# The matmuls of the convolution's LayerNorm sums, two steps further down in TensorE's queue

## The chip, the cores and the metric

The kernel runs on one core of a Trainium2 chip. The metric is the device time of one execution in microseconds (us), lower is better. TensorE (PE in the profile) does the matmuls, VectorE (DVE), ScalarE (ACT) and GpSimd (POOL) the elementwise work, and SyncE (SP) issues the weight loads. Each engine takes its own instructions in the order in which the program wrote them.

## The reference, cut to what matters

Two layers over 256 tokens of width 2048. Layer 0 mixes retention heads and latent attention heads. Layer 1, where the change lies, is a convolution module:

```python
def layer_conformer_conv(x, norm_g, w_in, conv_w, conv_b, ln_g, ln_b, w_out):
    h = rms_norm(x, norm_g)
    a, b, gate = jnp.split(h @ w_in, 3, axis=-1)
    u = a * jax.nn.sigmoid(b)
    u = causal_depthwise_conv_31(u, conv_w) + conv_b      # 31 taps per channel
    u = jax.nn.silu(layer_norm(u, ln_g, ln_b))            # mean and variance over 2048 channels
    return x + (u * jax.nn.silu(gate)) @ w_out
```

The LayerNorm needs, for each token, the sum and the sum of squares over all 2048 channels of the convolution's output. Only then can the first column of the last product, `@ w_out`, be worked out.

## The kernel before, in words

Everything is held with channels on the partitions and tokens along the free dimension: 16 blocks of 128 channels by 256 tokens. Each float32 product is done as three matmuls on rounded parts (`mm3`, L190 to L195): high weight by high activation, high weight by low activation, low weight by high activation. So every weight block has to be split on the chip: ScalarE writes the rounded part `whi` (`hi_to`, L161), and VectorE or GpSimd writes the remainder `wlo` (`lo_to`, L171). The buffers are rings: 3 of `raw` (the loaded weights), 5 of `whi`, 4 of `wlo`.

**Steps.** The weights come in halves of a 1 MB unit. `Stream.half` (L180) is called ahead of each half. It writes the instructions for the remainder `wlo` three halves ahead and for `whi` four halves ahead, then sets the kernel's own clock to the next whole number and lets due work run (`tick`, L108). In the middle of a half a second tick advances it by another half (`tick(True)`), and due work can come there too. One half feeds 24 matmuls of 128x128 by 128x256. In this text one half is called a step. A wlo buffer three steps ahead reuses the one that the step before the present one has read, so its VectorE instruction can start only when TensorE has finished that step.

**Delayed work.** `later(n, fn)` (L102) puts a function down for n steps after now. Each `tick` runs what has come due, ordered by due time and then by the order of putting down, and so writes its instructions into the engines' queues at that place. The order of the queues on TensorE, ScalarE and VectorE is thus written by hand, by such lags.

**The stretch around the change.** While TensorE works out the 16 pairs of `a` and `b` columns and then the 8 pairs of gate columns (`pair`, L352, four steps each, loop at L1096), VectorE runs the convolution's 31 taps per block (L91) as a background, a few at each tick (`pace`, L919). When the last block is done, `centre_add` (L950) adds it to the running sums, writes the result to `sums` (in tile `e`), and puts down `norm_conv` for `LN_LAG` steps later (L958).

`norm_conv` (L984) has two matmuls by a matrix of ones, L986 and L987, that add the 128 partitions up. They are float32, recorded as two passes each. Behind them come the mean, the variance and the reciprocal root on VectorE and ScalarE (from L989 on, `rs_chain`, with a table load at L994). Then 8 pairs of blocks j = 0 to 7 go through five stages each, half a step apart, and pair j starts 2j steps after `norm_conv`:

```python
def za(j): ...  # DVE: subtract the mean, multiply by the root (two instructions)
def zs(j): ...  # ACT: silu with gain and bias (L1008, two instructions)
def zb(j): ...  # DVE: multiply by the gate
def zr(j): ...  # ACT: rounded part zh (L1017)
def zc(j): ...  # DVE: remainder zl
for j in range(8):
    later(2 * j, lambda j=j: z_run(j, 0))
```

After the last pair of gate columns the output projection begins. Its first part is a group of 16 steps with 8 column blocks held at once (`kgroup` on `u_co1`, L1129): step k multiplies by block k of z, so it needs pair j = k//2. The first block's matmuls are lines L345 and L348, the others L193 to L195 into `aux`. `z_need` (L1044) would write missing stages at once; it writes none here if the lags have already brought them. The second part (`u_co2`, pairs again) has 8 x 4 steps of matmuls over all 16 blocks, with the adds and stores at the end.

The steps are numbered from the start of that group: step 0 is its first, steps -4 to -1 are the last gate pair (pair 7), -8 to -5 the pair before it (pair 6). In the kernel before, the sums are written at the tick that opens step -7, and `norm_conv` comes due 2.5 steps later, in the middle of step -5, with 12 + 4 x 24 = 108 matmuls between it and step 0. At the end of a pair, `norm_cols` (L1066) multiplies its result by the RMS factor on VectorE, and the gate's silu on ScalarE follows one step later. A gate that comes due after the sums are written and before `norm_conv` is held until `norm_conv` runs (L1105), so that the ScalarE tables aren't changed in between.

Of the kernel before, what the change touches and what calls it, by code (L numbers as in the profile page):

```python
# [27 lines left out]
TAP_US = 0.396  # L28
TICK_US = 2.88
X1_US = 5.0  # L30
LN_LAG = 2.5
WARM = 9
ENG = {mybir.EngineType.PE, mybir.EngineType.Activation, mybir.EngineType.DVE}
MAGIC = 12582912.0
# [14 lines left out]
def body(ctx, tc, a):  # L49
# [52 lines left out]
    def later(n, fn):  # L102
        due.append((clock[0] + n, len(due), fn))
# [846 lines left out]
    def centre_add(c, m):  # L950
# [4 lines left out]
        if c == 15:  # L955
            lnexp()
            held.append([])
            later(LN_LAG, norm_conv)  # L958

# [267 lines left out]
```

## Time and profile before

| what | value |
|---|---|
| time, median of 3 runs | 840.26 us (838.32 to 843.09) |
| the profiled execution's own time | 839.34 us |
| its span, first to last instruction | 837.6 us |
| granted TensorE clock, mean | 0.995 |
| TensorE's longest wait | 4.3 us, at L986 |

The span and all rows of the trace belong to the one profiled execution. Outside its span lie 839.34 - 837.6 = 1.74 us. The timeline lists instructions by start, length, engine and line; several of a kind in a row are merged with a count, and an idle time ahead of an instruction stands in brackets with what ended it.

### The profile page before, as it was taken

What the parts mean: (1) busy time and instruction counts of PE and PEld (TensorE: products, weight loads), DVE (VectorE), ACT (ScalarE), POOL (GpSimd) and SP (SyncE); (2) the same over time, 40 slices, a digit from 0 to 9 for tenths busy, and PEclk for the clock granted to TensorE, in tenths of its full rate; (3) what the DMA queues carried; (4) which work ended last, traced back from release to release, by engine and by line L of the source; (5) the groups of instructions that cost most, each with busy time, mean ns of one, the idle gap of its engine ahead of it and who ended that gap; (6) DMA issues with size and microseconds to landing.
All of it is one profiled execution on the core that took longest, in us unless ns stands there. A gap on an engine that the chain in (4) does not pass through costs nothing.

```text
span 837.6 us, 16060 instructions
## 1 busy us (share of the span) xinstructions
PE 826.2 (99%) x6592; PEld 814.5 (97%) x6592; DVE 632.5 (76%) x1151; ACT 422.0 (50%) x593; POOL 207.5 (25%) x115
## 2 busy tenths in 40 slices
PE   9999999999999999999999999999999999799998
PEld 8999999999999999999999999999999999799998
DVE  5887565798587755765666399999999999898542
ACT  6766444556455554754545544434444543576330
POOL 0000000000000000000001888885988884000000
PEclk9999999999999999999999999999999999899999
DMA  8965554434545344655444555553555555355650
GB/s 263 350 242 177 185 187 166 151 133 174 197 138 187 133 147 137 218 200 203 171 168 164 201 193 168 195 189 114 201 202 200 177 178 178 125 182 195 228 176 26
DMA packets 24122, 151.16 MB, mean 180 GB/s; under 512 B 2801, under 2 KB 3953, under 8 KB 6897
## 3 DMA queue, kind: packets, MB, share of 16 engines
q1 hardware_dynamic: 23616, 148.03, 51.1%
q0 software_dynamic: 288, 2.10, 0.7%
q8 instruction: 51, 0.84, 0.4%
q14 instruction: 23, 0.18, 0.1%
q10 hardware_dynamic: 144, 0.03, 0.0%
HBM read 148.04 MB, written 2.10 MB: 179 GB/s over the span
## 4 chain that ended last, share of the span: by engine, by line
PE 76%; DVE 20%; issue 1%; ACT 1%; DMA 1%; POOL 1%; SPq 0%; DVEq 0%; POOLq 0%; ACTq 0%
PE mm L195 22%; PE mm L193 22%; PE mm L194 22%; DVE aux L91 13%; DVE mm L88 2%; DVE s L88 2%; PE aux L195 2%; PE aux L194 2%; PE aux L193 2%; DVE wlo L88 1%; DVE t L88 1%; DMA raw<-in_w_first 1%; POOL wlo L88 1%; ACT whi L167 0%; PE aux L641 0%
## 5 line engine op out<-in xcount | busy, mean ns | idle before, releaser
L193 PE MATMUL mm<-s,whi 128*128 128x256 f32 x1788 | 511.0, 286 | 0.5 <-ACT whi L167 0.5
L195 PE MATMUL mm<-s,wlo 128*128 128x256 f32 x1788 | 507.2, 284 | 1.8 <-POOL wlo L88 1.0
L194 PE MATMUL mm<-s,whi 128*128 128x256 f32 x1788 | 506.6, 283 | 0.0
L167 ACT ACTIVATE whi<-raw 128x1024 fp32r<-128x1024 f32 (+2 forms) x278 | 283.2, 1034 | 200.7 <-PE mm L194 121.1
L195 PEld LDWEIGHTS mm<-s,wlo 128*128 128x128 f32 x1788 | 343.7, 192 | 2.9 <-DVE wlo L88 1.6
L193 PEld LDWEIGHTS mm<-s,whi 128*128 128x128 f32 x1788 | 343.8, 192 | 1.5 <-ACT whi L167 0.7
L194 PEld LDWEIGHTS mm<-s,whi 128*128 128x128 f32 x1788 | 343.9, 192 | 0.8
L88 DVE TENSOR_TENSOR wlo<-raw,whi 128x1024 fp32r<-128x1024 f32 (+2 forms) x194 | 229.4, 1193 | 87.3 <-PE mm L195 52.3
L88 POOL TENSOR_TENSOR wlo<-raw,whi 128x1024 fp32r<-128x1024 f32 x84 | 201.9, 2415 | 44.5 <-ACT whi L167 21.9
L91 DVE SCALAR_TENSOR_TENSOR aux<-s,cb,aux 128x256 f32<-128x256 f32 x478 | 198.6, 481 | 11.7 <-ACT aux L872 9.0
L691 POOL MEMSET s<- 64x256 f32 x8 | 2.9, 361 | 232.6 <-PE mm L195 162.7
L193 PE MATMUL mm<-whi,s 128*128 128x272 f32 (+1 forms) x184 | 59.3, 322 | 0.0
L194 PE MATMUL mm<-wlo,s 128*128 128x272 f32 (+1 forms) x184 | 58.9, 320 | 0.0
L195 PE MATMUL mm<-whi,s 128*128 128x272 f32 (+1 forms) x184 | 58.8, 319 | 0.0
L195 PEld LDWEIGHTS mm<-whi,s 128*128 128x128 f32 x184 | 34.6, 188 | 2.3
L193 PEld LDWEIGHTS mm<-whi,s 128*128 128x128 f32 x184 | 34.7, 189 | 1.8
L194 PEld LDWEIGHTS mm<-wlo,s 128*128 128x128 f32 x184 | 34.6, 188 | 1.8
L193 PE MATMUL aux<-s,whi 128*128 128x256 f32 x120 | 34.0, 283 | 0.0
L194 PE MATMUL aux<-s,whi 128*128 128x256 f32 x120 | 34.0, 283 | 0.0
L195 PE MATMUL aux<-s,wlo 128*128 128x256 f32 x120 | 34.0, 283 | 0.0
L1076 ACT ACTIVATE t<-mm 128x256 f32<-128x256 f32 x16 | 6.1, 384 | 54.9 <-DVE mm L88 54.9
L855 POOL MEMSET s<- 128x30 f32 x16 | 1.1, 121 | 119.4 <-PE mm L195 103.6
(186 smaller groups left out, 574.8 us busy)
## 6 DMA issues: line engine op xcount, KB each, us to landing
raw<-in_c_in SPq DMA_DIRECT2D x48, 1024.0 KB, 4.9
raw<-in_w_in SPq DMA_DIRECT2D x36, 1024.0 KB, 4.9
raw<-in_w_out SPq DMA_DIRECT2D x16, 1024.0 KB, 4.9
raw<-in_c_out SPq DMA_DIRECT2D x16, 1024.0 KB, 4.8
raw<-in_w_rv SPq DMA_DIRECT2D x8, 1088.0 KB, 5.0
raw<-in_w_kvb SPq DMA_DIRECT2D x4, 1024.0 KB, 4.9
raw<-in_w_first SPq DMA_DIRECT2D x7, 512.0 KB, 5.5
raw<-in_w_qb SPq DMA_DIRECT2D x3, 1024.0 KB, 4.9
```

Source lines behind the costliest of these rows:

```text
L88: (eng or V).tensor_tensor(out=out, in0=in0, in1=in1, op=op)
L91: V.scalar_tensor_tensor(out=out, in0=in0, scalar=s, in1=in1, op0=op0, op1=op1)
L167: act(hi[:, :], self.raw[u][:, h * n:(h + 1) * n], AF.Copy)
L193: mm(ps, lh, rh, start=start, stop=False, skip_group_check=True)
L194: mm(ps, lh, rl, start=False, stop=False, skip_group_check=True)
L195: mm(ps, ll, rh, start=False, stop=stop, skip_group_check=True)
L691: G.memset(krz(i)[64 * b:64 * b + 64, :], 0.0)
L855: G.memset(upad(c, 0, TAPS - 1), 0.0)
L1076: act(sg[0][:, 0:T], ps[:, T:512], AF.Sigmoid)
```

## The change

One constant, the lag between the writing of the sums and `norm_conv`, goes from 2.5 to 4.5 steps:

```diff
 TAP_US = 0.396
 TICK_US = 2.88
 X1_US = 5.0
-LN_LAG = 2.5
+LN_LAG = 4.5
 WARM = 9
```

`norm_conv` now comes due in the middle of step -3 in place of the middle of step -5. With it move all that it writes or puts down: the two sum matmuls, the chain behind them on VectorE and ScalarE, and all five stages of the 8 pairs. What is put down elsewhere keeps its place: the taps, the sums, `norm_cols`, the splitting of the weights. The gate of pair 6 comes due in the middle of step -4, which is now ahead of `norm_conv`, so it is held and written right behind the chain.

## The prediction

> **What bounds the kernel now.** The first view is the page's head with the busy times.
>
> ```profile
> span 837.6 us, 16060 instructions
> PE 826.2 (99%) x6592; PEld 814.5 (97%) x6592; DVE 632.5 (76%) x1151; ACT 422.0 (50%) x593; POOL 207.5 (25%) x115
> ```
>
> TensorE sets the time: 11.4 us of 837.6 are left uncovered. So only what makes TensorE wait or run slowly counts. The second view is TensorE's waits from 690 us on, and the third the windows around the one wait that it lists (columns: stretch, length, busy time and count of PE, PEld, DVE, ACT, POOL, then granted clock, DMA share, GB/s).
>
> ```profile
> PE aux L986 <- DVE e L88: 4.3, 1, 4.3
> 720.60:725.10 4.50, 0.25 (x3) 0.04 (x2) 3.92 (x9) 0.86 (x3) 0.00 (x0) 0.84 0.49 206
> 725.10:731.00 5.90, 5.90 (x25) 5.54 (x26) 4.21 (x7) 3.94 (x5) 0.00 (x0) 0.54 0.51 178
> ```
>
> TensorE stands 4.3 us at the sum matmuls, until VectorE has written the sums. The wait has a second price: the mean clock of 0.84 over the wait means that it went to one half for (1 - 0.84) / 0.5 x 4.5 = 1.4 us of it, so it fell at 723.7, 2.8 us after the last matmul. In the next window 0.54 means half speed for (1 - 0.54) / 0.5 x 5.9 = 5.4 us after the restart. The fourth view is TensorE's timeline.
>
> ```profile
> 720.44 0.28 PE L194 MATMUL mm<-s,whi 128*128 128x256 f32 x1
> 720.56 0.28 PE L195 MATMUL mm<-s,wlo 128*128 128x256 f32 x1
> 725.09 1.22 PE L986 MATMUL aux<-e,ones 128*128 128x256 f32 x2 [4.25 <-DVE e L88]
> ...
> 726.60 0.78 PE L193 MATMUL mm<-s,whi 128*128 128x256 f32 x1
> ...
> 729.95 0.41 PE L195 MATMUL mm<-s,wlo 128*128 128x256 f32 x1
> 730.16 0.41 PE L193 MATMUL mm<-s,whi 128*128 128x256 f32 x1
> ...
> 741.47 2.08 PE L345 MATMUL aux<-s,whi 128*128 128x256 f32 x16
> ```
>
> Starts are 0.12 us apart at full clock and 0.21 at half; a step of 24 is 24 x 0.12 = 2.88 us. Step 0, the first that needs z, starts at 741.47. The fifth view is VectorE's timeline from the last taps to the first z.
>
> ```profile
> 720.71 1.22 DVE L88 TENSOR_TENSOR wlo<-raw,whi 128x1024 fp32r<-128x1024 f32 x1
> ...
> 725.06 0.42 DVE L88 TENSOR_TENSOR e<-mm,t 128x256 f32<-128x256 f32 x1
> 725.40 1.22 DVE L88 TENSOR_TENSOR wlo<-raw,whi 128x1024 fp32r<-128x1024 f32 x1
> 727.43 1.22 DVE L88 TENSOR_TENSOR wlo<-raw,whi 128x1024 fp32r<-128x1024 f32 x1 [0.81 <-ACT whi L167]
> 728.57 0.41 DVE L989 TENSOR_SCALAR t<-aux 128x256 f32<-128x256 f32 x1
> ...
> 732.42 0.68 DVE L88 TENSOR_TENSOR s<-s,t 128x512 f32<-128x512 f32 x1
> 733.14 0.69 DVE L88 TENSOR_TENSOR s<-s,e 128x512 f32<-128x512 f32 x1
> 733.75 0.69 DVE L88 TENSOR_TENSOR mm<-mm,R 128x512 f32<-128x512 f32 x1
> 734.35 1.21 DVE L88 TENSOR_TENSOR wlo<-raw,whi 128x1024 fp32r<-128x1024 f32 x1
> 735.48 0.68 DVE L88 TENSOR_TENSOR s<-s,s 128x512 f32<-128x512 f32 x1
> 736.08 1.22 DVE L88 TENSOR_TENSOR wlo<-raw,whi 128x1024 fp32r<-128x1024 f32 x1
> 737.22 0.68 DVE L88 TENSOR_TENSOR s<-s,t 128x512 f32<-128x512 f32 x1
> 737.93 0.69 DVE L88 TENSOR_TENSOR s<-s,e 128x512 f32<-128x512 f32 x1
> 738.55 0.68 DVE L88 TENSOR_TENSOR s<-s,s 128x512 fp32r<-128x512 f32 x1
> ```
>
> The reader sees a VectorE that is hardly idle: between these rows it stood for 0.81 us, and otherwise ran one instruction after the other or the chain behind L989. By the order in which the program writes them, the remainders at 720.71, 725.40, 727.43, 734.35 and 736.08 are those for steps -4, -3, -2, -1 and 0. The sums end at 725.06 + 0.42 = 725.48. The last row is zc of pair 0: z for step 0 is there at 738.55 + 0.68 = 739.23, and TensorE comes for it at 741.47, only 2.2 us later. So TensorE's wait in front of L986 hides a second lateness of VectorE, and that is what the change lays open.
>
> **The change, part by part.** TensorE first. Its stall at 720.7 goes: the 12 matmuls left in step -5 run from 720.68, step -4 from 722.12 to 725.00 (its remainder is there at 720.71 + 1.22 = 721.93). Step -3 starts at 725.00, but its third matmul, at 725.24, needs the remainder that ends at 725.40 + 1.22 = 726.62. A new wait of 1.4 us, then, shorter than the 2.8 us after which the clock fell above, so I take no clock loss for it. Ten more matmuls bring TensorE to the sum matmuls at 727.9; the sums have been there since 725.48. These took 726.60 - 725.09 = 1.5 us at half clock; at full clock I take half of it, 0.75. Then 60 matmuls are left to step 0, 60 x 0.12 = 7.2 us. TensorE arrives at step 0 at 727.9 + 0.75 + 7.2 = 735.8, or 736.6 if the sums still take 1.5. That is 5.6 us earlier than 741.47, which is the gross gain: the 4.3 us of waiting, and 2.7 us of half clock, less the 1.4 us.
>
> Now VectorE, with the new order in its queue. Nothing is different up to 727.43. Behind that remainder came the chain; now there stand ahead of it three instructions that came later before: the `norm_cols` of pair 6 (734.35 - 733.75 = 0.60), the remainder of step -1 (735.48 - 734.35 = 1.13) and that of step 0 (737.22 - 736.08 = 1.14). Their inputs are ready: step -5 ends at 722.1, and ScalarE has room for the rounded parts, as its timeline shows.
>
> ```profile
> 726.34 2.00 ACT L167 ACTIVATE whi<-raw 128x1024 fp32r<-128x1024 f32 x2
> ...
> 732.44 1.06 ACT L167 ACTIVATE whi<-raw 128x1024 fp32r<-128x1024 f32 x1
> 733.87 1.09 ACT L1008 ACTIVATE s<-s,cb 128x256 f32<-128x256 f32 x2 [0.36 <-DVE s L88]
> 734.87 0.57 ACT L1102 ACTIVATE s<-mm 128x512 f32<-128x512 f32 x1
> ```
>
> Two rounded parts end at 728.3, two more at 1.0 each at 730.4, and the loads for them were made before. So L989 starts at 728.57 + 0.60 + 1.13 + 1.14 = 731.4, where it was at 728.57. The chain up to za takes 732.42 - 728.57 = 3.85: za at 735.3. za takes 733.75 - 732.42 = 1.33: 736.6. The remainder of step 1 follows, 1.13: 737.8. zs on ScalarE needs za (ready at 736.7) and stands behind the chain's table load (the rounded part behind it started at 732.44 before, so the load ends 2.87 us later than that, at 735.3), the held gate (0.57) and a rounded part (1.06): it starts at 736.9 and ends at 738.0. zb 0.60: 738.6. The remainder of step 2, 1.13: 739.7. za of pair 1, 738.55 - 737.22 = 1.33: 741.1. zc of pair 0, 0.68: 741.75. So z for step 0 comes at 741.75, 2.5 us later than before, because two more remainders (steps 1 and 2) stand in front of it. TensorE, there at 735.8, waits until 741.75, with one matmul (the one that needs only zh) let through a little sooner. Against 741.47 + 0.12, where the second matmul of step 0 ran before, that is **+0.15 us**: the whole gross gain is gone at step 0.
>
> The new wait is 5.9 us, longer than the 4.25 us one. The clock fell 2.8 us into that one, so here too; and I take the same 5.4 us of half speed after the restart, as this is the only such restart in the trace. Step 0 then costs 24 x (0.21 - 0.12) = **+2.2 us**. The bounds: nothing if the clock holds, and 2.2 for a longer half speed as well, since what of it falls into step 1 is hidden by the next part.
>
> A second new cost is in steps 1 to 12. Pair j's zc is now written in the middle of step 2j - 1 and needed at step 2j; before there were two and a half steps between. On VectorE there stand ahead of it the remainder for three steps on, which cannot start before TensorE has finished step 2j - 2, and za of the next pair. The trace of before shows just that sequence, at the beginning of its step 7 (741.47 + 7 x 2.88 = 761.63).
>
> ```profile
> 760.90 0.69 DVE L88 TENSOR_TENSOR s<-s,s 128x512 f32<-128x512 f32 x1 [0.54 <-ACT s L1008]
> 761.83 1.22 DVE L88 TENSOR_TENSOR wlo<-raw,whi 128x1024 fp32r<-128x1024 f32 x1 [0.23 <-PE aux L195]
> ...
> 764.30 0.68 DVE L88 TENSOR_TENSOR s<-s,s 128x512 fp32r<-128x512 f32 x1
> ```
>
> The remainder waits for TensorE (0.23 in brackets), and zc ends at 764.30 + 0.68 = 764.98, 3.35 us after the step's start; with 0.05 for the signal, 3.40. The next step's second matmul would run at 2.88 + 0.12 = 3.00. So each odd step gets 0.40 us longer wherever zc gates: j = 2 to 6, 5 x 0.40 = **+2.0 us**. For j = 1, step 1 still has 5.4 - 24 x 0.21 = 0.3 us of half clock in it, which takes some 0.15 of the 0.40 away: **+0.3**, with rounding. Pair 7 has no za of a next pair ahead of it, 0.20 + 1.13 + 0.68 = 2.0 us after the step's start, and costs nothing. Even steps hold only the remainder and zb: the 760.90 row ends at 761.59, before step 7 starts. Behind step 14 nothing of the change is left, and TensorE has no other wait that could give time back.
>
> GpSimd has no instruction in the stretch, and the loads keep their order on SP: each waits for the remainder that empties its buffer, which comes sooner than before (steps -1 and 0) or at most some 2 us later (1 and 2), with 4 steps to spare. The load of steps 2 and 3 goes out when the remainder of step -3 has emptied its buffer, at 726.6 as before.
>
> Sum: 0.15 + 2.2 + 0.3 + 2.0 = 4.65, say **+4.7 us**. On the profiled execution's 839.34 us (1.74 of them outside the span) that gives 844.0; the median of the runs is 0.9 higher, 840.26, so I forecast **845.0 us**, 0.56% slower. A measurement of this kernel can tell about 0.5%, 4.2 us, from no change.
>
> [...] When the clock comes back decides on which side of 4.2 us the sum falls. By the rows it fell at 723.7 and was back at 725.10 + 5.4 = 730.5, 6.8 us apart. [...]
>
> **The rivals.**
>
> *The wait goes and nothing follows* (faster). TensorE runs on into step 0 at 735.8: -5.6 us, 834.6. For it speaks that L986 is the only wait in the list. It decides at z for step 0 being ready by 735.8, but before the change, with the chain unmoved in VectorE's queue, it was ready at 739.23. To be there at 735.8 VectorE would have to pass the remainders, which the order of its queue doesn't let it. Chance 0.05.
>
> [...] Chance 0.22.
>
> *The clock holds* (no change). Then 0.15 + 6 x 0.40 = 2.55: 842.8. [...] Chance 0.06.
>
> *The steps keep up* (no change). If VectorE gets through the odd steps 0.4 us faster, the lag per pair is gone, and 0.15 + 2.2 = 2.35 is left: 842.6. Against it: the step 7 rows. Chance 0.10.
>
> *The lag is larger* (slower still). If zb of an even step, too, is held up by zs on ScalarE (the 0.54 in brackets), each pair costs 0.8: 2.4 us more, 847.4. Chance 0.10.
>
> **How the numbers follow.** My forecast as worked out has 0.47 left; its own size is from 844.0 to 846, and I put 0.02 of it under the bound. Slower by over 0.5% is then 0.45 + 0.10 = 0.55; within it 0.02 + 0.22 + 0.06 + 0.10 = 0.40; faster 0.05. The range reaches from 841.3, the case of 842.6 less 1.3 for the spread of the runs (838.32 to 843.09 around 840.26), to 848.0, the case of 847.4 with a little of it.
>
> **What would show it.** Right: no wait at L986; a wait of some 1.4 us at a remainder in step -3; L989 near 731.4; a wait of 5 to 6 us at step 0 (L345, released by VectorE's s), and a clock near one half behind it; then six waits of about 0.3 to 0.4 us at even steps 2 to 12. Step 0 would start near 741.7 and step 14 some 4.7 us later than before. Wrong: step 0 starting before 739, or no wait there at all; a full clock behind the wait; no waits at the even steps; or L989 still near 728.6.

## The result and the profile after

The changed kernel takes 845.43 us (median; 844.89 to 846.64), the kernel before 840.26 us (838.32 to 843.09) next to it: a ratio of 1.0068 (95% interval 1.0057 to 1.0079), 5.7 us on 840.26. The ratio is not that of the two medians, which lie 5.2 us apart. Run again beside the kernel before, the same change came to 1.0070 (1.0057 to 1.0084).

The page's head after the change:

```profile
span 843.1 us, 16057 instructions
PE 827.4 (98%) x6592; PEld 814.5 (97%) x6592; DVE 633.4 (75%) x1151; ACT 421.3 (50%) x593; POOL 207.5 (25%) x115
```

The span has grown by 843.1 - 837.6 = 5.5 us. TensorE's uncovered time went from 11.4 to 15.7 us, 4.3 of the 5.5; its busy time grew by 1.2, with the same 6592 matmuls. In the rows below, a matmul next to a wait counts as busy for 0.28 to 0.39 us, while in a stream they start 0.12 apart, and there are more waits now. No engine got more work. TensorE's waits from 690 us on show where the time lies:

```profile
PE aux L345 <- ACT s L1017: 3.2, 1, 3.2
PE aux L345 <- DVE s L88: 1.9, 1, 1.9
PE aux L194 <- DVE s L88: 1.5, 6, 0.3
PE mm L195 <- DVE wlo L88: 1.3, 1, 1.3
```

The 4.3 us at L986 are gone from the list. In their place stand a remainder in step -3 (1.3), step 0 in two pieces (3.2 until zh is there, then one matmul, then 1.9 until zl is), and six short waits at `aux` matmuls L194. TensorE's timeline has the places:

```profile
726.78 0.39 PE L195 MATMUL mm<-s,wlo 128*128 128x256 f32 x1 [1.34 <-DVE wlo L88]
728.08 0.60 PE L986 MATMUL aux<-e,ones 128*128 128x256 f32 x2
...
739.47 0.38 PE L345 MATMUL aux<-s,whi 128*128 128x256 f32 x1 [3.17 <-ACT s L1017]
741.80 3.57 PE L345 MATMUL aux<-s,whi 128*128 128x256 f32 x15 [1.94 <-DVE s L88]
...
750.24 0.39 PE L194 MATMUL aux<-s,whi 128*128 128x256 f32 x1 [0.26 <-DVE s L88]
750.46 0.28 PE L195 MATMUL aux<-s,wlo 128*128 128x256 f32 x1
...
756.51 0.38 PE L194 MATMUL aux<-s,whi 128*128 128x256 f32 x1 [0.25 <-DVE s L88]
...
781.57 0.38 PE L194 MATMUL aux<-s,whi 128*128 128x256 f32 x1 [0.25 <-DVE s L88]
```

The sum matmuls now start without a wait. The second matmul of step 0 starts at 741.80, against 741.59 before. The last of the six short waits ends at 781.57, the second matmul of step 12. Before, that place was 741.47 + 12 x 2.88 + 0.12 = 776.15, so 5.4 of the span's 5.5 us are lost by there. VectorE's timeline has the cause:

```profile
725.51 1.22 DVE L88 TENSOR_TENSOR wlo<-raw,whi 128x1024 fp32r<-128x1024 f32 x1
...
728.69 0.69 DVE L88 TENSOR_TENSOR mm<-mm,R 128x512 f32<-128x512 f32 x1
729.29 2.35 DVE L88 TENSOR_TENSOR wlo<-raw,whi 128x1024 fp32r<-128x1024 f32 x2
731.55 0.42 DVE L989 TENSOR_SCALAR t<-aux 128x256 f32<-128x256 f32 x1
...
741.06 0.69 DVE L88 TENSOR_TENSOR s<-s,s 128x512 fp32r<-128x512 f32 x1
```

The row at 725.51 is the remainder of step -3, 725.40 before: this execution got there 0.11 us later. The three instructions that now stand ahead of L989 are plain to see, `norm_cols` and the remainders of steps -1 and 0. L989, whose first matmul began at 728.08, runs at 731.55; z of pair 0 is ready at 741.06 + 0.69 = 741.75, and 0.05 us later TensorE goes on. The windows before and after that restart:

```profile
735.90:741.80 5.90, 0.79 (x6) 0.39 (x4) 5.81 (x9) 5.09 (x9) 0.00 (x0) 0.84 0.48 157
741.80:747.70 5.90, 5.90 (x31) 5.90 (x32) 2.95 (x4) 2.64 (x4) 0.00 (x0) 0.58 0.58 197
```

In windows of 1 us the clock reads 1.00 from 718 to 739, 0.96 up to 740, 0.50 up to 746, 0.62 up to 747 and 1.00 up to 757 (in the kernel before 1.00 up to 723, 0.84, 0.50 from 724 to 730, 0.75, and 1.00 from 731 on to 743). So half clock lasted (1 - 0.84) / 0.5 x 5.9 = 1.9 us of the wait and (1 - 0.58) / 0.5 x 5.9 = 5.0 us behind it. In the first window, where TensorE was busy for 0.79 us, VectorE was busy for 5.81 of the 5.90.

### The profile page after: what moved, and what is told of

Read it like the earlier page. It is cut to its first block, busy times and chain, and to the rows that moved or that the text cites. A ratio compares the mean times of both kernels' runs of the same rounds, so it can differ in the third digit from the quotient of the medians.

```text
span 843.1 us, 16057 instructions
## 1 busy us (share of the span) xinstructions
PE 827.4 (98%) x6592; PEld 814.5 (97%) x6592; DVE 633.4 (75%) x1151; ACT 421.3 (50%) x593; POOL 207.5 (25%) x115
## 4 chain that ended last, share of the span: by engine, by line
PE 86%; DVE 11%; ACT 1%; DMA 1%; issue 1%; POOL 1%; SPq 0%; DVEq 0%; POOLq 0%; ACTq 0%
PE mm L195 26%; PE mm L194 26%; PE mm L193 26%; DVE s L88 3%; DVE aux L91 3%; DVE wlo L88 2%; PE aux L194 1%; PE aux L195 1%; DVE t L88 1%; PE aux L193 1%; DMA raw<-in_w_first 1%; DVE mm L88 1%; POOL wlo L88 1%; ACT whi L167 0%; PE aux L345 0%
## 5 line engine op out<-in xcount | busy, mean ns | idle before, releaser
L195 PE MATMUL mm<-s,wlo 128*128 128x256 f32 x1788 | 506.6, 283 | 3.1 <-DVE wlo L88 2.1
L194 PE MATMUL mm<-s,whi 128*128 128x256 f32 x1788 | 505.8, 283 | 0.0
L195 PEld LDWEIGHTS mm<-s,wlo 128*128 128x128 f32 x1788 | 342.9, 192 | 4.3 <-DVE wlo L88 3.1
L194 PEld LDWEIGHTS mm<-s,whi 128*128 128x128 f32 x1788 | 343.0, 192 | 0.7
L194 PE MATMUL mm<-wlo,s 128*128 128x272 f32 (+1 forms) x184 | 58.9, 320 | 0.0
L195 PE MATMUL mm<-whi,s 128*128 128x272 f32 (+1 forms) x184 | 58.8, 319 | 0.0
L195 PEld LDWEIGHTS mm<-whi,s 128*128 128x128 f32 x184 | 34.6, 188 | 2.3
L194 PEld LDWEIGHTS mm<-wlo,s 128*128 128x128 f32 x184 | 34.6, 188 | 1.8
L194 PE MATMUL aux<-s,whi 128*128 128x256 f32 x120 | 34.6, 288 | 1.5 <-DVE s L88 1.5
L195 PE MATMUL aux<-s,wlo 128*128 128x256 f32 x120 | 33.9, 283 | 0.0
```

What stands on the lines that cost most here:

```text
L194: mm(ps, lh, rl, start=False, stop=False, skip_group_check=True)
L195: mm(ps, ll, rh, start=False, stop=stop, skip_group_check=True)
```

## The experiments

Each was run beside the kernel before on the same chip, and the ratios are to that: the first four on one chip (7 to 12 executions each, 30 of the kernel before), the last on another (5 and 9). The change itself was not run beside the first four. Numbers in us are the ratio times 840.26; their intervals reach about 1 us to either side. A table of all runs stands at the end of this section.

**One step less.** The constant alone:

```diff
-LN_LAG = 4.5
+LN_LAG = 3.5
```

> Lag 3.5, one step short of the change. Theory (VectorE's queue makes z late, by what stands ahead of it): L989 near 730.3, behind norm_cols and one remainder; TensorE waits 1.9 us at L986 in the middle of step -4, no clock loss there; z of pair 0 at 740.6, so step 0 about 1.0 us earlier than in the kernel before, behind a wait of some 4 us; no waits at the even steps 2 to 12, as 1.5 steps lie between zc and its use. Time: 841.5 if the clock falls at step 0 (-1.0 + 2.2 + 0.2), 839.3 if it holds. Rival (the loss grows evenly with the lag): half of the change's loss, 842.9. Rival (only the wait at L986 counts): 837 or less.

Measured: 1.0018 (1.0006 to 1.0030), +1.5 us or 841.8; the theory had 841.5 or 839.3, the even growth 842.9, just outside the interval. VectorE's timeline, TensorE's, two windows, and TensorE's waits from 700 us on, all of them:

```profile
728.39 0.69 DVE L88 TENSOR_TENSOR mm<-mm,R 128x512 f32<-128x512 f32 x1
728.99 1.22 DVE L88 TENSOR_TENSOR wlo<-raw,whi 128x1024 fp32r<-128x1024 f32 x1
730.12 0.42 DVE L989 TENSOR_SCALAR t<-aux 128x256 f32<-128x256 f32 x1
```

```profile
724.91 0.70 PE L986 MATMUL aux<-e,ones 128*128 128x256 f32 x2 [1.35 <-DVE e L88]
...
738.04 0.38 PE L345 MATMUL aux<-s,whi 128*128 128x256 f32 x1 [1.93 <-ACT s L1017]
740.37 2.77 PE L345 MATMUL aux<-s,whi 128*128 128x256 f32 x15 [1.94 <-DVE s L88]
```

```profile
740.37:745.00 4.63, 4.63 (x26) 4.63 (x27) 4.59 (x6) 3.57 (x5) 0.00 (x0) 0.63 0.54 214
741.00:743.00 2.00, 2.00 (x13) 2.00 (x13) 2.00 (x4) 1.71 (x3) 0.00 (x0) 0.60 0.82 348
```

```profile
PE aux L345 <- DVE s L88: 1.9, 1, 1.9
PE aux L345 <- ACT s L1017: 1.9, 1, 1.9
PE aux L986 <- DVE e L88: 1.4, 1, 1.4
```

One remainder and `norm_cols` stand ahead of L989, and it starts at 730.12, between the 728.57 of before and the 731.55 of the change. The second matmul of step 0 starts at 740.37, earlier than in either. No even step waits. So with 1.5 steps between zc and its use the lag per pair is gone, and what is left is the clock: half speed for (1 - 0.63) / 0.5 x 4.63 = 3.4 us. That is 3.4 / 0.21 = 16 matmuls at 0.09 each, 1.5 us, in place of the 2.2 of the expectation; counted from the remainder of step -3, step 0 starts 1.0 us earlier than before, which leaves some +0.5 in this execution. The rest of the +1.5 is not explained by this trace. The loss does not grow evenly with the lag: +1.5 us for the first step, over 4 for the second.

**zc ahead of the next za.** Lag 4.5; a pair's last stage starts the next pair, in place of a due time of its own:

```diff
-        for j in range(8):
-            later(2 * j, lambda j=j: z_run(j, 0))
+        later(0, lambda: z_run(0, 0))
...
             later(0.5, lambda: z_run(j, s + 1))
+        elif j < 7:
+            z_run(j + 1, 0)
```

> Lag 4.5, but each pair's zc is written ahead of the next pair's za, in the same tick. Theory: z of pair 0 comes 1.3 us sooner (740.4), the waits at steps 2 to 12 go, since zc is then over 2.0 us after the odd step's start; the clock still falls at step 0. Time: 845.4 - 1.3 - 5 x 0.5 - 0.3 = 841.3. Rival (the even steps wait for the weight ring or for ScalarE, not for the order on VectorE): only the 1.3 us go, 844.1, and the six waits stay.

Measured: 1.0015 (1.0006 to 1.0025), +1.3 us or 841.5, where 841.3 was expected and 844.1 by the rival. TensorE's waits from 700 us on, all of them:

```profile
PE aux L345 <- ACT s L1017: 3.2, 1, 3.2
PE mm L195 <- DVE wlo L88: 1.3, 1, 1.3
PE aux L345 <- DVE s L88: 0.6, 1, 0.6
```

The window behind step 0's second matmul:

```profile
740.23:746.00 5.77, 5.77 (x35) 5.77 (x36) 4.79 (x7) 3.15 (x5) 0.00 (x0) 0.70 0.56 199
```

The six waits are gone, with the same remainders at the same places of the queue, and the wait for zl at step 0 is 1.3 us shorter, which is za's time. So those waits came from the order of za and zc on VectorE. The weight ring does set when a remainder can start (in the change's trace the one at 753.30 stood for 0.75 us until TensorE was through with L195), but alone it kept no step of this run waiting. Not all of the gain is the missing waits: half speed behind the restart was (1 - 0.70) / 0.5 x 5.77 = 3.5 us here, where it was 5.0 in the change.

**TensorE kept busy ahead of step 0.** Lag 4.5, and matmuls on ones into an unused bank where TensorE would wait:

```diff
+    busy = mmps()
+    for _ in range(22):
+        nc.tensor.matmul(busy[:, 0:P], ones[:, :], ones[:, :], start=True, stop=True)
     banks = kgroup(u_co1, 8, 2, zrhs, bank=auxps)
```

> Lag 4.5, with 22 matmuls of ones by ones (128 columns, into an unused PSUM bank) ahead of step 0, to fill TensorE's wait of 5.5 us there; they add nothing to the result. Theory: the clock stays at full, step 0 takes 2.9 us in place of 5.1, step 1 then has the full lag of 0.5 in place of 0.2; step 0 itself starts where it did (741.8), as VectorE sets it. Time: 845.4 - 2.2 + 0.3 = 843.5. Rival (half speed at step 0 is hidden behind VectorE's next pair anyway): no change, 845.4.

Measured: 1.0039 (1.0025 to 1.0053), +3.3 us or 843.5, as expected. Its waits, the window up to step 0, and two rows of TensorE's timeline, the second matmuls of steps 0 and 2:

```profile
PE aux L194 <- DVE s L88: 1.5, 6, 0.3
PE mm L195 <- DVE wlo L88: 1.3, 1, 1.3
PE aux L345 <- DVE s L88: 0.5, 1, 0.5
```

```profile
735.30:741.02 5.72, 5.26 (x47) 5.06 (x46) 5.63 (x9) 4.91 (x8) 0.00 (x0) 1.00 0.45 155
```

```profile
741.02 2.05 PE L345 MATMUL aux<-s,whi 128*128 128x256 f32 x15 [0.46 <-DVE s L88]
...
747.28 0.39 PE L194 MATMUL aux<-s,whi 128*128 128x256 f32 x1 [0.25 <-DVE s L88]
```

The clock stays at 1.00 (1.00 from 741.02 to 746.00 as well), the six waits stay, and doing useless work in the gap saves 5.7 - 3.3 = 2.4 us. That is the price of the clock alone, as a difference of two ratios that were measured separately. The traces bear it out: between the two rows lie 6.26 us, and in the change 750.24 - 741.80 = 8.44, 2.2 more. Step 0 itself does not come sooner: its second matmul stands 16.3 us behind the start of the remainder of step -3 in both (741.02 - 724.74 and 741.80 - 725.51).

**Both.** Lag 4.5, zc first, and 18 such matmuls:

> Lag 4.5, zc ahead of the next za, and 18 filling matmuls ahead of step 0. Theory: of the change's loss only the place of step 0 is left: z of pair 0 at 740.4, no half clock, no waits at the even steps. Step 0's second matmul at 740.5 against 741.6 before: -1.1, some 0.1 to 0.3 of leftover waits. Time: 839.3, just under the kernel before. Rival (something else in the late chain costs time): over 841.

Measured: 0.9996 (0.9985 to 1.0006), -0.3 us or 839.9. The only wait left on TensorE's list is the remainder in step -3:

```profile
PE mm L195 <- DVE wlo L88: 1.3, 1, 1.3
```

The two edits take away 6.0 us, the change's whole 5.7 and 0.3 more. The rival of another hidden cost in the late chain, over 841, falls: the interval ends at 840.8. The time is 0.6 above the expected one, which lies within the interval.

**An order made from the theory.** The sums at the opening of step -3, and the queues of VectorE and ScalarE behind them written by need: first what z of pair 0 needs, with each remainder just ahead of the step that reads it.

```diff
-LN_LAG = 4.5
+LN_LAG = 4.0
...
-            self.lo_to(j + 3)
-            self.hi_to(j + 4)
+            self.lo_to(min(j + self.la, self.lo_cap))
+            self.hi_to(min(j + self.ha, self.hi_cap))
...
+        act(y, y, AF.Exp, scale=-0.5)
...
+        st.lo_to(first0 - 2)
+        st.hi_to(first0)
...
+        za(0)
+        zs(0)
+        st.lo_to(first0 - 1)
+        zb(0)
+        zr(0)
+        zc(0)
+        za(1)
...
+        later(1, lambda: z_run(1, 1))
+        for j in range(2, 8):
+            later(2 * j - 1.5, lambda j=j: z_run(j, 0))
```

`la` and `ha` are 3 and 4 as before, and 2 and 3 from `norm_conv` on. The caps hold remainders behind that of step -3, and rounded parts behind that of step -1, back between the sums and `norm_conv`. `norm_cols` of pairs 6 and 7 goes with their gates, which come some steps later.

> A version made from the theory: norm_conv at the tick that opens step -3 (lag 4.0), and VectorE's queue ordered behind the sums: remainder of step -3, then the chain with the remainder of step -2 in its gap, za of pair 0, remainder of step -1 beside zs, zb, zc of pair 0 and za of pair 1, and only then the remainders of steps 0 on, written two steps ahead in place of three; norm_cols and the gates of pairs 6 and 7 come later, and ScalarE's rounded parts are held back likewise. Theory: TensorE waits about 0.5 us at L986, up to 1 us for the remainder of step -1, z of pair 0 is there at about 735, step 0 starts near 735.7 with the clock at full, some 0.7 us of waits at remainders after it: 5 us less than the kernel before, a ratio near 0.994. Rival (VectorE has no room: 10 us of its work lie between the sums and z of pair 0 however they are ordered, and what is put off comes back): z of pair 0 not before 738, or the waits come back at steps 1 to 6; ratio 0.998 or above.

Measured: 835.16 us against 839.32, a ratio of 0.9953 (0.9940 to 0.9965), -3.9 us. It is faster than both kernels. The second line of its page, its waits, and VectorE's timeline (the lines of this kernel are numbered a little higher: L197 is L195 of the others, L993 is L989, L1030 is L1017):

```profile
PE 824.7 (99%) x6592; PEld 812.1 (97%) x6592; DVE 632.2 (76%) x1151; ACT 421.4 (51%) x593; POOL 207.5 (25%) x115
```

```profile
PE mm L197 <- DVE wlo L88: 0.6, 2, 0.4
PE aux L197 <- DVE wlo L88: 0.4, 1, 0.4
```

```profile
726.52 1.22 DVE L88 TENSOR_TENSOR wlo<-raw,whi 128x1024 fp32r<-128x1024 f32 x1
727.65 0.42 DVE L993 TENSOR_SCALAR t<-aux 128x256 f32<-128x256 f32 x1
...
735.59 0.69 DVE L88 TENSOR_TENSOR s<-s,s 128x512 fp32r<-128x512 f32 x1 [0.70 <-ACT s L1030]
```

From the remainder of step -3 to the end of zc of pair 0 it takes 735.59 + 0.69 - 726.52 = 9.8 us; in the change it took 741.75 - 725.51 = 16.2 us. The engine and its instructions are the same as a whole; in the new order `norm_cols`, three remainders and za of pair 1 no longer stand in this stretch. What is left are three waits of 1.0 us together. The rival, that VectorE has no room, falls: the work put off did not come back as waits. The ratio is 0.0013 above the 0.994 that was expected, at the end of the interval.

**All runs side by side.** The traces give a second measure. Executions reach the remainder of step -3 at different times, so this table counts from its start to the end of the span. What the edits change in VectorE's queue lies behind it.

| kernel | remainder of step -3 starts | span | from there to the end | against before | by the ratio |
|---|---|---|---|---|---|
| before | 725.40 | 837.6 | 112.2 | | |
| the change | 725.51 | 843.1 | 117.6 | +5.4 | +5.7 |
| the change, run again | 724.93 | 841.9 | 117.0 | +4.8 | +5.9 |
| one step less | 725.22 | 837.9 | 112.7 | +0.5 | +1.5 |
| zc first | 725.29 | 837.8 | 112.5 | +0.3 | +1.3 |
| TensorE kept busy | 724.74 | 840.1 | 115.4 | +3.2 | +3.3 |
| both | 726.98 | 838.0 | 111.0 | -1.2 | -0.3 |
| order by need | 726.52 | 833.9 | 107.4 | -4.8 | -3.9 |

This is one execution each, all set against the same one of the kernel before. The two measures differ by up to 1.1 us, so smaller differences between the runs are not shown; the conclusions above hold by either.

## Why the prediction was right

The forecast was 845.0 us, 0.56% slower; measured were 845.43 us and 0.68%. The two traces are 0.11 us apart at the remainder of step -3; the comparisons below leave that in unless they say otherwise. The mechanism came as forecast, piece by piece.

- *L986's wait goes, and step -3 gets one of 1.4 us for a remainder.* Both: 1.34 at 726.78.
- *L989 near 731.4, behind three instructions.* 731.55, of which 0.11 is the traces' offset. The run with lag 3.5, with one remainder fewer ahead, has 730.12.
- *z of pair 0 at 741.75, +0.15 us at step 0.* 741.75, and the second matmul at 741.80 against 741.59, +0.2. TensorE had been through with step -1 at 739.47 - 3.17 = 736.3, some 5 us earlier than before, and gave all of it back there.
- *The clock falls, +2.2 us, with +0.3 at step 1.* From 741.80 to 750.24 are 8.44 us, against 2 x 2.88 = 5.76 before: 2.7 for the two steps, forecast 2.5. The filled gap shows the clock's own part by experiment, 2.4 us by the ratios and 2.2 by the traces. That the size fits so well is in part luck. The forecast had the clock fall 2.8 us into the wait and stay low for 5.4 us behind it. It fell at 741.80 - 1.9 = 739.9, 3.6 us after TensorE went idle at 736.3, with one matmul in between, and half speed lasted 5.0 us behind the restart. When the change was run again, the same two steps took 749.08 - 741.21 = 7.87 us, a loss of 2.1.
- *Five lags of 0.40, +2.0 us.* This term was too small: from 750.24 to 781.57 are 31.33 us for ten steps, against 28.8 before, so 2.53, or 0.51 each. zc did come at the predicted place. What was left out is that the matmul behind the one that waited started 0.22 us after it and not 0.12 (750.24 to 750.46, and 0.22 or 0.23 at the other five): 0.10 per wait.
- *A VectorE that stood for 0.81 us only.* The reading passed over 0.45 us at 722.78, where it waited for ScalarE ahead of the sums. That wait is the same in both traces (722.89 in the change) and enters no term.

The terms measured are 0.2 + 2.7 + 2.5 = 5.4, the forecast's 4.7 and 0.5 for the lags and 0.2 for the clock. That the order of VectorE's queue is the cause was only read from the program in the forecast. The run with zc first changes nothing but that order, and the waits that it should end are gone. The order by need changes the lag and ScalarE's order as well, so it shows that the room was there, not what each of its edits is worth.

Of the rivals, the clean gain is out: L986 waits no more, and the time is longer. A clock that is back well before the forecast's 5.4 us did not come in the change's trace (half speed for 5.0 us behind the restart), but did in the run with lag 3.5 (3.4 us in all) and in the one with zc first (3.5), so it was a fair rival. A clock that holds is out (0.58 behind the restart), and so is the larger lag (0.8 a pair, where 0.51 was measured). The weaker one, steps that keep up, is what the run with zc first has by design.

## What to carry to other kernels

A wait on the busiest engine is worth moving only if what it feeds is early enough: ask first when the result at the other end of the chain is ready, and what stands in the queues between. Here an instruction moved by two steps on TensorE moved its whole chain behind three foreign instructions on VectorE, and took from the pairs of stages the slack that had hidden a fixed order of theirs. The fastest run kept the sums late, at the opening of step -3, and put the late engine's queue in order; what that order would be worth with the sums in their old place was not run.

## What the runs showed that was not expected

In two runs the clock fell after TensorE had gone back to work. In the one with lag 3.5 the window 740.37 to 745.00 holds 3.4 us of half speed, and the window 741.00 to 743.00 has 0.60, 1.6 us of it: the clock fell at about 741.4, 1.0 us after the restart at 740.37, and was back 3.4 us on. TensorE had stopped at 738.04 - 1.93 = 736.1, and until the fall it was busy for 0.38 us at 738.04 and for 1.0 from 740.37 on. In the run with zc first the clock is 0.97 from 740 to 741, 0.06 us of half speed: it fell at 740.9, 0.7 us after the restart at 740.23. In the profiled executions of the change and of the kernel before it fell inside the wait and stayed low for 1.9 + 5.0 = 6.9 and 1.4 + 5.4 = 6.8 us. What sets these times is not shown by the traces.

So half speed behind the restart lasted from 3.4 to 5.4 us here, with the kernel before included. What it costs differed between two executions of one kernel as well, as the change run again shows:

```profile
741.21 3.57 PE L345 MATMUL aux<-s,whi 128*128 128x256 f32 x15 [1.75 <-DVE s L88]
...
749.08 0.39 PE L194 MATMUL aux<-s,whi 128*128 128x256 f32 x1 [0.26 <-DVE s L88]
```

Its two steps lost 0.6 us less than those of the first trace. Of the 30 executions of the kernel before on the chip of the first four experiments, three have a mean clock of 0.993 and a mean span of 839.6 us, twelve 0.995 and 837.5, six 0.997 and 836.6, nine 0.998 and 837.1. The lowest clock goes with the longest span; among the others the spans do not follow the clock. With the order by need all five executions show 1.000.
